# A fixed 56-step plan for the work woven into attention, and one modulation chunk moved to VectorE

## The chip, the cores and the metric

One core of one Trainium2 chip runs the whole program. The metric is the device time of one execution in microseconds. Three runs of the kernel before took 1927.2 us in the median (1920.5 to 1932.17).

The engines named below: TensorE (PE) multiplies matrices into PSUM, and its weight loads (PEld) run beside its products; VectorE (DVE), ScalarE (ACT) and GpSimd (POOL) work on tiles; SyncE (SP) issues the DMAs from one queue.

## What is computed

A block of two layers over 512 latent tokens and a context prefix of 256 tokens, model width 1024. Layer 0 mixes tokens by grouped-query attention (16 heads of 64, 4 key heads), layer 1 by a bidirectional Mamba-2 scan. Each layer ends with a gated feed-forward network of width 2816 with a depthwise convolution (FFN 0 and FFN 1). Shift, scale and gate of every sub-layer come from a linear map of the condition, for latent and for context rows: six chunks of 1024 numbers for each layer, for each of two conditions. Cut to what bears on the change:

```python
for i in range(DEPTH):
    need_ctx_out = i < DEPTH - 1
    mod_l = jnp.split((silu_c @ ada_w[i] + ada_b[i])[:, None, :], 6, axis=-1)
    mod_c = jnp.split(silu_cc @ ada_w[i] + ada_b[i], 6, axis=-1)
    h_l = modulate(rms_norm(x, norm_mix_w[i]), mod_l[0], mod_l[1])
    h_c = modulate(rms_norm(ctx, norm_mix_w[i]), mod_c[0], mod_c[1])
    ...
    x = x + mod_l[2] * o_l
    if need_ctx_out:
        ctx = ctx + mod_c[2] * o_c
    h_l = modulate(rms_norm(x, norm_ffn_w[i]), mod_l[3], mod_l[4])
    x = x + mod_l[5] * conv_ffn(h_l, ...)
    if need_ctx_out:
        h_c = modulate(rms_norm(ctx, norm_ffn_w[i]), mod_c[3], mod_c[4])
        ctx = ctx + mod_c[5] * conv_ffn(h_c, ...)
return x
```

In layer 1 the context stream ends after the mixer's input, so its chunks 2 to 5 for context rows (`mod_c[2]` to `mod_c[5]`) are read by nothing.

## The kernel before

Activations lie transposed, features on the 128 partitions, tokens along the free axis. Every product with a weight is made three times, from a high and a low part of both factors (`mm3`, L105, L106, L108); a weight of 128 x 1024 is loaded by SP, its high part is a cast on ScalarE (L85) and its low part a subtraction (L87), on VectorE or, with `lo_engine="pool"`, on GpSimd. Weights and the modulation's slabs share one pool of 10 tiles (`t4`); a load waits until a tile is free.

**Attention** runs its eight head pairs in seven steps each, 56 in all. A step makes the scores of one key tile (L686, L688), their exponential on ScalarE (L689), a running sum on VectorE (L694, L696), the products with the values of the step before (L650), and one piece of the next pair's row maxima: a product (L614) and a reduction on VectorE (L616). `final` closes a pair: sums on TensorE (L656), then VectorE and ScalarE (L659 to L663). The scores and the maxima share two PSUM buffers.

**Woven into the steps** are other jobs, as Python generators that `Fill` advances. After each step `fill.run(us)` spends a budget of 1.75 us (2.9 us in the last two pairs) by going through the queue in order and drawing from each generator as long as budget is left; a `BREAK` rests a generator for some steps. The queue is `"123a4k5a6a7aaaaa"`:

- digits are `queries(p)`: for pairs 4 to 7 load and split of the weight, 16 units of products (`ps_q`), and for all pairs the chain `normed`: a square and a scaling on ScalarE (L527, L528), four small SBUF-to-SBUF loads that swap rows (`qsw`, L531), the rotary products (L532 to L534) on the engine that the caller names, GpSimd here, sums of squares on TensorE (L540), and the normalisation (L546 to L552); last the split into a high and a low part;
- `k` is the same chain for the second pair of key heads (`keys(1)`);
- each `a` is one of eight modulation jobs `ada` for chunks 2 to 5 of layer 0: four loads of 512 KB, 8 products (`ps_ada`, L128), a copy to SBUF (L130), 4 transposes (`ps_adt`, L134), the bias added (`modulation`).

`fill.require` runs to its end what the next pair needs. Pairs 0 to 5 write their output to DRAM (`odram`). In the first step of pair 6 five of them are fetched back and split (`osplit`) and two output projections are queued (`late`, `project`: groups (0,1,2) and (3,4) of `w_o`), each adding to `X` on VectorE (`down`, L797). The group (5,6,7) follows behind the attention, merged with the first products of FFN 0.

Instructions of all engines are placed by a scheduler that takes the program's order as priority; on its engine, an instruction runs in the order so found.

**FFN 0** (`ffn`): 22 blocks of two products each (`up`: gate, then value), convolution and gating on VectorE and ScalarE, and `down` in groups of blocks (`segs`: nine of 2, one of 1, one of 3), whose updates multiply by `mod[0][5]`. Between them `side` puts the modulation of layer 1 on VectorE: `ada_dve` sums each of 48 loaded tiles against the latent and the context condition (L167, 96 sums), one sum at each place.

Of the kernel before, what the change touches and what calls it, by code (L numbers as in the profile page):

```python
# [7 lines left out]
P = 128  # L8
# [102 lines left out]
def ada(g, src, layer, chunks, m0, nm, big=True):  # L111
# [23 lines left out]
    for i, ch in enumerate(chunks):  # L135
        modulation(g, pt[:, 2 * nm * i : 2 * nm * (i + 1)], layer, ch, m0, nm)
# [3 lines left out]
def modulation(g, ps, layer, ch, m0, nm):  # L140

    nc = g.nc
    c0 = PC[f"adab{layer}"] + ch * KT + m0
    md = g.mod[layer][ch][:, m0 : m0 + nm, :]
    nc.vector.tensor_tensor(md, ps.rearrange("p (m v) -> p m v", v=2),
                            g.par[:, c0 : c0 + nm].unsqueeze(2).broadcast_to([P, nm, 2]), ALU.add)
    if ch in (1, 4):
        n0 = PC[("nmix" if ch == 1 else "nffn") + str(layer)] + m0
        nc.vector.scalar_tensor_tensor(g.moda[layer][ch][:, m0 : m0 + nm, :], md, 1.0,
                                       g.par[:, n0 : n0 + nm].unsqueeze(2).broadcast_to([P, nm, 2]),  # L150
                                       ALU.add, ALU.mult)


def ada_dve(g, layer):
# [5 lines left out]
    for ch in range(6):  # L160
        md = g.mod[layer][ch]
        for m in range(KT):
            w = g.t3p.tile([P, D], F32, tag="wada", bufs=3, name="wada")
            nc.sync.dma_start(w, g.I["adaT"][ch * KT + m])
            for v in range(2):
                junk = g.t3p.tile([P, D], F32, tag="junk", bufs=1, name="junk")
                g.tc.keep_in_program_order(nc.vector.scalar_tensor_tensor(  # L167
                    junk, w, 1.0, cb[:, v * D : (v + 1) * D], ALU.mult, ALU.mult, accum_out=md[:, m, v : v + 1]))
                yield
        modulation(g, md.rearrange("p m v -> p (m v)"), layer, ch, 0, KT)  # L170
# [5 lines left out]
class Fill:  # L176

    def __init__(self):  # L180
        self.q, self.cool, self.left = [], {}, 0.0

    def add(self, gen):
        self.q.append(gen)

    def run(self, us):

        self.left = min(self.left, 0.0) + us
        self.cool = {g: n - 1 for g, n in self.cool.items() if n > 1}
        for g in list(self.q):  # L190
            while self.left > 0 and g not in self.cool:
                r = next(g, None)
                if r is None:
                    self.q.remove(g)
                    break
                if r is BREAK:
                    self.cool[g] = 3
                    self.left -= 1.0
                else:
                    self.left -= r  # L200

    def require(self, gen):
        for _ in gen:
            pass
        if gen in self.q:
            self.q.remove(gen)

    def drain(self):
        for g in self.q:
            for _ in g:  # L210
                pass
        self.q = []
# [166 lines left out]
def attention(g, fill, X, late):  # L379
# [144 lines left out]
    def normed(qs, gain, eng):  # L524
# [7 lines left out]
        eng.tensor_tensor(qs[:, :L], qs[:, :L], g.cos, ALU.mult)  # L532
        eng.tensor_tensor(sw, sw, g.sin, ALU.mult)
        eng.tensor_tensor(qs[:, :L], qs[:, :L], sw, ALU.add)  # L534

# [6 lines left out]
        yield BREAK  # L542
# [10 lines left out]
        yield BREAK  # L553
# [3 lines left out]
    def keys(j, qs, eng):  # L557
        yield from normed(qs, kn, eng)
# [9 lines left out]
        yield 0  # L568
# [3 lines left out]
    def queries(p, qs, eng):  # L572
        if qs is None:
            w = load_w(g, I["wq"][p - 4], lo_engine="pool")
            yield BREAK
            qs = t3(g, "qs")
            for h, c0, n in ((hc, L, C), (hl, 0, L)):
                ps = Bk("ps_q")
                for k in range(KT):
                    ks = slice(k * P, (k + 1) * P)  # L580
                    mm3(g, (w[0][:, ks], w[1][:, ks]), [(ps[:, :n], h[k])], k == 0, k == KT - 1)
                    yield 3 * n / 2400
                nc.scalar.copy(qs[:, c0 : c0 + n], ps[:, :n])
            yield BREAK
        yield from normed(qs, g.qn8, eng)
        qprep[p] = t3(g, "qh", F32R), t3(g, "ql", F32R)
        split(g, qs, *qprep[p])
        yield 0
# [118 lines left out]
    for n, j in enumerate((0, 1, 2, 4, 5, 3)):  # L707
# [6 lines left out]
        if n in (1, 2):  # L714
            early.append(keys(0, raw[0], nc.vector) if n == 1 else queries(0, raw[1], nc.vector))
# [7 lines left out]
    qgen = {p: queries(p, raw[{1: 2, 2: 4, 3: 5}[p]] if p < 4 else None, nc.gpsimd) for p in range(1, 8)}  # L723
    kgen = keys(1, raw[3], nc.gpsimd)

    g.oT = []
    odram = [g.dp.tile([P, T], F32, name=f"odram{p}") for p in range(6)]

    def osplit(p):
        hl_, hc_ = htiles(g, L, f"ol{p}"), htiles(g, C, f"oc{p}")  # L730
        o = g.o[p]
        if p < 6:
            o = t3(g, f"od{p}")
            nc.sync.dma_start(o, odram[p])
        split(g, o[:, :L], *hl_)
        split(g, o[:, L:T], *hc_)
        g.oT.append((hl_, hc_))

    adas = list(fill.q)
    fill.q = [kgen if o == "k" else adas.pop(0) if o == "a" else qgen[int(o)] for o in "123a4k5a6a7aaaaa"]  # L740
    g.o = []
    pairs = [Pair(p) for p in range(NH // 2)]

    m = pairs[0].maxima()
    for i, _ in enumerate(vals):
        if i % 5 == 0:
            next(m, None)
        if i % 6 == 5:
            next(qgen[1], None)
    for _ in m:  # L750
        pass
    late_step = None
    for p in range(NH // 2):
        m = iter(())
        if p < 7:
            fill.require(qgen[p + 1])
            if p == 3:
                fill.require(kgen)
            m = pairs[p + 1].maxima()
        us = 1.75 if p < 6 else 2.9  # L760
        for t, todo in enumerate(pairs[p].steps()):
# [694 lines left out]
```

## Time and profile before

| what | value |
|---|---|
| median of 3 runs | 1927.2 us |
| the profiled execution: its span | 1929.7 us |
| bytes read from HBM | 198.79 MB |
| DMA, share of 16 engines' time | 34.0% |

The page gives the execution's span, from the first to the last instruction, and no other time of it. An engine's share is its busy time over the span. A busy TensorE is not one at its peak: products are pipelined, and the clock that it is granted is a row of its own. In the timeline's rows the bracket gives the idle time ahead of an instruction and what ended it.

### The profile page before, as it was taken

What the parts mean: (1) busy time and instruction counts of PE and PEld (TensorE: products, weight loads), DVE (VectorE), ACT (ScalarE), POOL (GpSimd) and SP (SyncE); (2) the same over time, 40 slices, a digit from 0 to 9 for tenths busy, and PEclk for the clock granted to TensorE, in tenths of its full rate; (3) what the DMA queues carried; (4) which work ended last, traced back from release to release, by engine and by line L of the source; (5) the groups of instructions that cost most, each with busy time, mean ns of one, the idle gap of its engine ahead of it and who ended that gap; (6) DMA issues with size and microseconds to landing.
All of it is one profiled execution on the core that took longest, in us unless ns stands there. A gap on an engine that the chain in (4) does not pass through costs nothing.

```text
span 1929.7 us, 27392 instructions
## 1 busy us (share of the span) xinstructions
PE 1877.4 (97%) x10744; PEld 1533.9 (79%) x10744; DVE 1337.2 (69%) x1976; ACT 844.2 (44%) x1446; POOL 312.5 (16%) x274
## 2 busy tenths in 40 slices
PE   8989999999999999999999999999999999999999
PEld 6755544678888888888888888888888878888887
DVE  5577777768777777775577777777878466555555
ACT  3655444345222222222256777766677343333331
POOL 2241101022000000000031334443335210000000
PEclk9989998999999999999999999999999999999999
DMA  8221343104434443332222444344343322323332
GB/s 334 77 88 37 124 150 128 45 23 143 128 123 131 131 131 122 121 95 62 68 92 63 132 117 124 110 131 120 106 136 120 99 77 88 109 88 101 97 99 87
DMA packets 73424, 210.00 MB, mean 109 GB/s; under 512 B 8912, under 2 KB 14416, under 8 KB 73168
## 3 DMA queue, kind: packets, MB, share of 16 engines
q1 hardware_dynamic: 73296, 208.26, 34.0%
q8 instruction: 84, 1.38, 0.3%
q14 instruction: 44, 0.36, 0.1%
HBM read 198.79 MB, written 6.82 MB: 107 GB/s over the span
## 4 chain that ended last, share of the span: by engine, by line
PE 77%; DVE 8%; ACT 4%; issue 3%; POOL 2%; DMA 2%; SPq 0%; POOLq 0%; DVEq 0%; ACTq 0%
PE ps_up L108 10%; PE ps_up L106 10%; PE ps_up L105 10%; PE ps_d L105 6%; PE ps_d L106 6%; PE ps_d L108 6%; PE ps_in L108 4%; PE ps_in L106 4%; PE ps_in L105 4%; PE ps_o L650 2%; PE ps_s L686 2%; PE ps_st L1043 2%; PE ps_wo L108 1%; DVE ht L281 1%; PE ps_wo L105 1%
## 5 line engine op out<-in xcount | busy, mean ns | idle before, releaser
L87 DVE TENSOR_TENSOR wl<-wst,wh 128x1024 fp32r<-128x1024 f32 x205 | 255.4, 1246 | 222.8 <-PE ps_up L106 110.1
L85 ACT CAST wh<-wst 128x1024 fp32r<-128x1024 f32 x211 | 221.2, 1049 | 411.7 <-DMA wst<-in_wup 336.6
L106 PE MATMUL ps_up<-hlf,wh 128*128 128x512 f32 x1008 | 357.1, 354 | 0.0
L105 PE MATMUL ps_up<-hhf,wh 128*128 128x512 f32 x1008 | 356.9, 354 | 0.0
L108 PE MATMUL ps_up<-hhf,wl 128*128 128x512 f32 x1008 | 356.8, 354 | 0.0
L106 PEld LDWEIGHTS ps_up<-hlf,wh 128*128 128x128 f32 x1008 | 190.6, 189 | 26.2
L105 PEld LDWEIGHTS ps_up<-hhf,wh 128*128 128x128 f32 x1008 | 190.6, 189 | 26.2
L108 PEld LDWEIGHTS ps_up<-hhf,wl 128*128 128x128 f32 x1008 | 190.5, 189 | 25.9
L105 PE MATMUL ps_in<-hhs,wh 128*128 128x512 f32 (+1 forms) x560 | 204.4, 365 | 0.0
L106 PE MATMUL ps_in<-hls,wh 128*128 128x512 f32 (+1 forms) x560 | 199.4, 356 | 0.0
L108 PE MATMUL ps_in<-hhs,wl 128*128 128x512 f32 (+1 forms) x560 | 198.7, 355 | 0.0
L105 PE MATMUL ps_d<-hdh,wh 128*128 128x512 f32 (+1 forms) x568 | 193.7, 343 | 1.4 <-DVE X L797 1.2
L108 PE MATMUL ps_d<-hdh,wl 128*128 128x512 f32 (+1 forms) x568 | 193.4, 341 | 0.0
L106 PE MATMUL ps_d<-hdl,wh 128*128 128x512 f32 (+1 forms) x568 | 192.9, 340 | 0.3 <-DVE hdl L87 0.3
L797 DVE SCALAR_TENSOR_TENSOR X<-ps_d,mod,X 128x512 f32<-128x512 f32 (+1 forms) x240 | 132.9, 588 | 20.8 <-PE ps_d L108 20.4
L106 PEld LDWEIGHTS ps_d<-hdl,wh 128*128 128x128 f32 x568 | 106.7, 188 | 15.5 <-DVE hdl L87 0.7
L105 PEld LDWEIGHTS ps_d<-hdh,wh 128*128 128x128 f32 x568 | 106.3, 188 | 15.4 <-DVE X L797 1.7
L105 PEld LDWEIGHTS ps_in<-hhs,wh 128*128 128x128 f32 x560 | 105.9, 189 | 15.1 <-issue 1.2
L167 DVE SCALAR_TENSOR_TENSOR junk<-wada,cb 128x1024 f32<-128x1024 f32 x96 | 117.2, 1220 | 1.1 <-ACT cb L159 0.9
L108 PEld LDWEIGHTS ps_in<-hhs,wl 128*128 128x128 f32 x560 | 105.8, 189 | 14.7
L108 PEld LDWEIGHTS ps_d<-hdh,wl 128*128 128x128 f32 x568 | 106.7, 188 | 13.3
L106 PEld LDWEIGHTS ps_in<-hls,wh 128*128 128x128 f32 x560 | 106.0, 189 | 13.2
(344 smaller groups left out, 3525.0 us busy)
## 6 DMA issues: line engine op xcount, KB each, us to landing
wst<-in_wup SPq DMA_DIRECT2D x88, 512.0 KB, 3.6
wada<-in_adaT SPq DMA_DIRECT2D x48, 512.0 KB, 3.6
wst<-in_win SPq DMA_DIRECT2D x48, 512.0 KB, 3.6
wst<-in_wdown SPq DMA_DIRECT2D x44, 512.0 KB, 4.2
wada<-in_adaB SPq DMA_DIRECT2D x32, 512.0 KB, 5.2
E<-ad SPq DMA_DIRECT2D x64, 256.0 KB, 7.3
ec<-ead SPq DMA_DIRECT2D x64, 128.0 KB, 5.1
wst<-in_wout SPq DMA_DIRECT2D x16, 512.0 KB, 3.5
```

Of the source, the lines that this page charges most:

```text
L85: keep(nc.scalar.copy(hi, src))
L87: keep(eng.tensor_tensor(lo, src, _r(hi), ALU.subtract))
L105: mm(out, wh, ah, start=first, stop=False)
L106: mm(out, wh, al, start=False, stop=False)
L108: mm(out, wl, ah, start=False, stop=last)
L167: g.tc.keep_in_program_order(nc.vector.scalar_tensor_tensor(junk, w, 1.0, cb[:, v * D : (v + 1) * D], ALU.mult, ALU.mult, accum_out=md[:, ...
L281: nc.vector.scalar_tensor_tensor(t[:, c0:c1], ap, g.moda[layer][ca][:, m, v : v + 1], rs[:, c0:c1], ALU.mult, ALU.mult)
L650: nc.tensor.matmul(po[S64[e], :n], v, pr[:, 512 * e + off : 512 * e + off + n], start=first, stop=last)
L686: nc.tensor.matmul(outs[e], a[S64[e], k], b[S64[e], q], start=i == 0, stop=False)
L797: nc.vector.scalar_tensor_tensor(ap, o[:, c0:c1], gate[:, m, v : v + 1], ap, ALU.mult, ALU.add)
L1043: nc.tensor.matmul(ps[:, d * 256 : (d + 1) * 256], Bt[:, t * P : (t + 1) * P], xw[d][t], start=t == ts[0], stop=t == ts[-1])
```

## The change

- `Fill` is replaced by `Weave`, which knows the 56 steps. At each step it takes all charges still open, divides them by the steps left, and spends that much. `Job`s are units of TensorE work with a charge; up to three places ahead in the list a job may do its loads. `Light`s are short pieces without products of weight (a part of a chain, one split), at most one at each step, with an earliest step and a condition. Loads of `w_o` and of the outputs are in a list of their own (`free`), three steps ahead of their splits.
- The rotary products and the query weights' low parts go from GpSimd to VectorE. In `normed` they stand behind the sums of squares.
- The weight of pair 4 is loaded ahead of the value loop and split at its unit 20; the chain of pair 1 is finished before the steps.
- The outputs are split one by one from step 31 on instead of five at once in the first step of pair 6; the projections are grouped (0,1), (2,3,4), then (5,6,7) as before.
- Six modulation jobs instead of eight run on TensorE. Chunk 5 of layer 0 is summed in `ada_dve`, ahead of layer 1, at two sums for each place in the first four blocks of FFN 0, so that it is there for the first `down`; the first group has 3 blocks, and the one of 1 is gone. Chunks 2 to 5 of layer 1 are summed for the latent condition alone: 16 + 32 + 32 = 80 sums instead of 96.

```diff
+    def step(self):
+        todo = sum(j.cost for j in self.jobs) + sum(it.cost for it in self.lights)
+        self.left = min(self.left, 0.0) + todo / max(1, self.steps - self.now)
+        self.left -= self.light()
+        for i, j in enumerate(self.jobs[:3]):
+            if i <= j.ahead:
+                j.start(self.now)
+        for j in list(self.jobs):
+            while self.left > 0 and j.cool <= self.now and not j.prep and j.ready():
+                r = next(j.units, None)
...
-    def normed(qs, gain, eng):
+    def normed(qs, gain):
...
-        eng.tensor_tensor(qs[:, :L], qs[:, :L], g.cos, ALU.mult)
-        eng.tensor_tensor(sw, sw, g.sin, ALU.mult)
-        eng.tensor_tensor(qs[:, :L], qs[:, :L], sw, ALU.add)
...
+        nc.vector.tensor_tensor(qs[:, :L], qs[:, :L], g.cos, ALU.mult)
+        nc.vector.tensor_tensor(sw, sw, g.sin, ALU.mult)
+        nc.vector.tensor_tensor(qs[:, :L], qs[:, :L], sw, ALU.add)
+        yield
...
-            w = load_w(g, I["wq"][p - 4], lo_engine="pool")
...
+    def wq_split(p):
+        wh, wl = t4(g, "wh", F32R), t4(g, "wl", F32R)
+        split(g, wq[p], wh, wl)
+        wq[p] = (wh, wl)
...
-    fill.q = [kgen if o == "k" else adas.pop(0) if o == "a" else qgen[int(o)] for o in "123a4k5a6a7aaaaa"]
...
+    weave = Weave(7 * len(pairs))
...
+        return Job(2.95, units(), lambda: next(gen), ahead=1)
...
+        jobs[p] = Job(8.35, q_units(p), lambda p=p: wq_load(p), lambda p=p: isinstance(wq.get(p), tuple))
...
+        jobs[fs] = Job(8 * len(fs) * 1.05, project(fs, wo), None,
+                       lambda fs=fs: all(f in g.oT and isinstance(wo.get(f), tuple) for f in fs))
...
+    weave.jobs = [jobs[4], a[0], jobs[5], a[1], jobs[6], a[2], jobs[7], a[3], a[4], a[5], jobs[0, 1], jobs[2, 3, 4]]
...
+        for i in range(3):
+            its.append(Light(lambda: next(gen, None), at, cost=0.0 if i else 1.45,
+                             ready=(lambda now: ready()) if i == 0 else
+                             (lambda now, b=its[i - 1], d=3 - i: b.when is not None and now >= b.when + d)))
...
+    wsplit = lambda p: Light(lambda: wq_split(p), 0, lambda now: jobs[p].began is not None and now >= jobs[p].began + 2)
+    q2, q3, kk = chained(2, 0), chained(3, 5), chained("k", 13)
+    qc = {p: chained(p, at, lambda p=p: jobs[p].done) for p, at in ((4, 9), (5, 20), (6, 29), (7, 36))}
...
-            if t == 0:
-                if p == 6:
-                    for i in range(5):
-                        osplit(i)
-                    late()
...
-            fill.run(us)
...
+    def place(f):
+        for _ in range(2 if f < 4 else 1):
+            next(side, None)
...
-    for n in [2] * 9 + [1, 3] if nxt else [2] * 11:
+    for n in [3] + [2] * 8 + [3] if nxt else [2] * 11:
...
-    for i in range(8):
-        fill.add(ada(g, I["adaB"][i], 0, (2 + i // 2,), 4 * (i % 2), 4))
+    adas = [ada(g, I["adaB"][i], 0, (2 + i // 2,), 4 * (i % 2), 4) for i in range(6)]
```

More of the change, by code (lines that the diff above doesn't have):

```diff
@@ L168, in ada_dve, with __init__, start @@
                     junk, w, 1.0, cb[:, v * D : (v + 1) * D], ALU.mult, ALU.mult, accum_out=md[:, m, v : v + 1]))
+                if layer == 0 and m == KT - 1 and v == 1 or layer and m == KT - 1 and v == nv - 1:
+                    break
                 yield
-        modulation(g, md.rearrange("p m v -> p (m v)"), layer, ch, 0, KT)
+        modulation(g, md[:, :, 0:nv], layer, ch, 0, KT, nv)
+        yield
 BREAK = object()
[L176 to L192, printed above, removed]
+class Job:
+    def __init__(self, cost, units, prep, ready=lambda: True, ahead=2):
+        self.cost, self.units, self.prep, self.ready, self.ahead = cost, units, prep, ready, ahead
+        self.began = None
+        self.cool, self.done = 0, False
+    def start(self, now=0):
+        if self.prep:
+            self.prep()
+            self.prep, self.began = None, now
@@ new lines, with __init__, light @@
+class Weave:
+    def __init__(self, steps):
+        self.jobs, self.lights, self.now, self.steps, self.left, self.n = [], [], 0, steps, 0.0, 0
+    def light(self):
+        for it in self.lights:
+            if it.at <= self.now and it.ready(self.now):
+                self.lights.remove(it)
+                it.run()
+                it.when = self.now
+                return it.cost
+        return 0.0
+    def step(self):
[8 more added lines that the diff above has]
+                r = next(j.units, None)
@@ L744, in attention @@
+    qfirst = chain[1]
+    jobs[4].start()
     m = pairs[0].maxima()
@@ L748, in attention @@
         if i % 6 == 5:
-            next(qgen[1], None)
+            next(qfirst, None)
+        if i == 20:
+            wq_split(4)
     for _ in m:
+        pass
+    for _ in qfirst:
         pass
```

189 lines of the change are left out of this document (113 added, 76 removed).

## The prediction

> **What bounds the kernel now.** I read the page first: the span, the engines' shares, the strip of the granted clock, the chain that ended last.
>
> ```profile
> span 1929.7 us, 27392 instructions
> PE 1877.4 (97%) x10744; PEld 1533.9 (79%) x10744; DVE 1337.2 (69%) x1976; ACT 844.2 (44%) x1446; POOL 312.5 (16%) x274
> ...
> PEclk9989998999999999999999999999999999999999
> ...
> PE 77%; DVE 8%; ACT 4%; issue 3%; POOL 2%; DMA 2%; SPq 0%; POOLq 0%; DVEq 0%; ACTq 0%
> ```
>
> TensorE is busy 97% of the span and makes 77% of the chain: a change is worth TensorE work taken out, or TensorE waits and slow clock taken out. The clock strip dips in slices of 48 us that include 96 to 145 and 289 to 338. So the view of windows is next, by stage: the attention steps run from 116 (first scores) to 411, FFN 0 from 460 to 975.
>
> ```profile
> 116.00:411.00 295.00, 279.20 (x1674) 157.41 (x1673) 219.40 (x302) 128.69 (x172) 41.73 (x25) 0.96 0.28 95
> ...
> 327.00:370.00 43.00, 42.24 (x239) 28.04 (x240) 35.41 (x54) 13.79 (x20) 0.00 (x0) 1.00 0.13 44
> ...
> 460.00:975.00 515.00, 514.78 (x2981) 454.30 (x2979) 360.69 (x556) 127.66 (x134) 0.11 (x1) 1.00 0.37 116
> ```
>
> Columns: length, then busy time of PE, PEld, DVE, ACT, POOL, then the granted clock. FFN 0 has 0.2 us of idle TensorE at full clock: nothing that leaves VectorE there can shorten it. The attention steps have 295.0 - 279.2 = 15.8 us of idle TensorE and a mean clock of 0.96. The timeline of TensorE gives the idle times with what ended them:
>
> ```profile
> 125.38 0.80 PE L686 MATMUL ps_s<-qh,kh 64*128 64x512 f32 x2 [4.09 <-ACT pr L689]
> 129.24 1.98 PE L650 MATMUL ps_o<-pr,v 128*64 128x512 f32 x4 [1.37 <-DVE qsq L550]
> ...
> 188.87 1.08 PE L656 MATMUL ps_sum<-acc,ones 128*64 128x512 f32 x4 [2.40 <-DVE qsq L550]
> ...
> 272.26 0.50 PE L686 MATMUL ps_s<-qh,kh 64*128 64x512 f32 x2 [2.06 <-ACT pr L689]
> ...
> 306.46 0.80 PE L614 MATMUL ps_m<-kh,qh 64*128 64x256 f32 x4 [2.62 <-DVE ma L616]
> ```
>
> These five are 12.54 us of the 15.8; the other 3.3 are shorter waits. The clock falls behind three of the five (windows of 4 us):
>
> ```profile
> 124.00:128.00 4.00, 2.50 (x10) 1.50 (x10) 2.65 (x1) 3.88 (x6) 3.51 (x2) 0.65 0.00 0
> 128.00:132.00 4.00, 2.76 (x8) 0.50 (x12) 4.00 (x6) 0.52 (x1) 0.00 (x0) 0.50 0.38 131
> 132.00:136.00 4.00, 4.00 (x20) 0.69 (x12) 1.77 (x3) 0.83 (x1) 0.00 (x0) 0.57 0.42 142
> ...
> 188.00:192.00 4.00, 3.13 (x16) 1.72 (x18) 3.72 (x8) 1.97 (x3) 0.00 (x0) 0.76 0.00 0
> 192.00:196.00 4.00, 4.00 (x20) 2.35 (x17) 3.59 (x7) 1.69 (x4) 0.00 (x0) 0.82 0.02 4
> ...
> 304.00:308.00 4.00, 1.53 (x5) 0.79 (x6) 4.00 (x5) 1.78 (x2) 0.00 (x0) 0.76 0.72 289
> 308.00:312.00 4.00, 4.00 (x16) 2.71 (x16) 2.55 (x4) 0.00 (x0) 0.00 (x0) 0.50 0.00 0
> 312.00:316.00 4.00, 4.00 (x11) 1.10 (x8) 1.90 (x3) 1.83 (x3) 0.00 (x0) 0.50 0.00 0
> ```
>
> Busy time times the missing clock: 2.50 x 0.35 + 2.76 x 0.50 + 4.00 x 0.43 = 4.0 us behind the first wait; 0.8 + 0.7 = 1.5 behind the third; 0.4 + 2.0 + 2.0 = 4.4 behind the last. So the five waits cost 12.5 + 9.9 = 22.4 us, and the attention steps are where time can be had.
>
> What made them, from the timeline of the other engines:
>
> ```profile
> 122.62 1.04 ACT L85 CAST wh<-wst 128x1024 fp32r<-128x1024 f32 x1 [1.86 <-DMA wst<-in_wq]
> ...
> 125.36 3.23 DVE L694 TENSOR_TENSOR acc<-pr 128x1024 f32<-128x1024 f32 x1 [1.51 <-ACT pr L689]
> ...
> 306.32 0.95 DVE L87 TENSOR_TENSOR ql<-qs,qh 128x768 fp32r<-128x768 f32 x1
> ```
>
> At 122.6 the cast of a query weight stood on ScalarE waiting for its load, with the step's exponential behind it; at the same time a VectorE addition took 3.23 us while GpSimd was busy 3.51 of 4.00. At 304 to 308 VectorE is busy 4.00 of 4.00: weight splits, a query split and the pair's own sums meet where five outputs and their weights are taken back at once.
>
> **The change, part by part.**
>
> ```profile
> 201.71 1.92 PE L128 MATMUL ps_ada<-wada,sc 128*32 128x512 f32 x16
> ...
> 209.13 1.08 PE L650 MATMUL ps_o<-pr,v 128*64 128x512 f32 x4
> ...
> 211.50 1.08 PE L650 MATMUL ps_o<-pr,v 128*64 128x512 f32 x4
> ...
> 213.94 1.05 PE L134 MATMUL ps_adt<-cst,ada_sb 128*128 128x2 f32 x8
> ...
> 217.21 1.03 PE L656 MATMUL ps_sum<-acc,ones 128*64 128x512 f32 x4
> ```
>
> *Two of eight modulation jobs leave TensorE.* One job is 1.92 us of products and 1.05 us of transposes, so 2 x 2.97 = 5.9 us of TensorE work leave a stage that TensorE bounds.
>
> *They come back in FFN 0* as 16 VectorE sums, at two per place for the first four blocks, and 32 sums for context rows that nothing reads are dropped.
>
> ```profile
> L167 DVE SCALAR_TENSOR_TENSOR junk<-wada,cb 128x1024 f32<-128x1024 f32 x96 | 117.2, 1220 | 1.1 <-ACT cb L159 0.9
> ```
>
> VectorE there gets 16 x 1.22 = 20 us more and 39 us less, in 515 us of which it works 361. Four blocks take four sums each instead of two: 8 x 1.22 = 9.8 us more in the first 60 us. TensorE's own 515 us cover it; I take 0, and 9.8 us as the upper end if it comes onto the path. Eight more loads of 512 KB go to a DMA share of 0.37. Grouping the down projection by three first and no group of one keeps every product and saves a pass of updates on VectorE, under the same cover: 0.
>
> *Spread and lookahead.* Query weights are loaded when the job is two places off and split two steps later; the early split lies in the value loop; output reloads and splits lie one per step instead of five at once; the three parts of a query's chain are set two and one steps apart. The waits at 125 and 306 have the two causes shown; those at 129 and 188 end with a step of a query's chain on VectorE (L550), that at 272 with an exponential that came late. All five are of work that the plan sets apart, so I count all 22.4 us as gone and leave the other 3.3 us as they are. What is late next is VectorE.
>
> *GpSimd's part moves to VectorE*: three rotary products for each of seven chains and four weight splits.
>
> ```profile
> L533 DVE TENSOR_TENSOR qsw<-qsw,cs x2: 680/684/687, 77.3 to 83.5; 128x512 f32<-128x512 f32 x2
> ...
> L87 DVE TENSOR_TENSOR wl<-wst,wh 128x1024 fp32r<-128x1024 f32 x205 | 255.4, 1246 | 222.8 <-PE ps_up L106 110.1 <-ACT wh L85 78.3 <-issue 17.3
> ```
>
> 21 x 0.684 + 4 x 1.246 = 19.3 us on VectorE: 219.4 + 19.3 = 239 us. In steps of 295 - 24 = 271 us that is 88%. From 327 to 370 VectorE was at 35.41 / 43 = 82% while TensorE lost 0.8 us at clock 1.00; 88% is somewhat beyond that row. Losing the collisions with GpSimd (3.23 us for an addition) gives some of it back; I count neither.
>
> *A wait is added.* The rotary products overwrite the tile that four small loads read, so VectorE waits for all four, and the pair's maxima and sums are queued behind; TensorE's next maxima wait for them. On GpSimd nothing stood behind it. In before, the first chain already runs on VectorE, ahead of the steps:
>
> ```profile
> 76.62 0.78 DVE L532 TENSOR_TENSOR raw<-raw,cs 128x512 f32<-128x512 f32 x1 [11.17 <-DMA qsw<-raw]
> ...
> 82.86 0.69 DVE L532 TENSOR_TENSOR raw<-raw,cs 128x512 f32<-128x512 f32 x1 [0.70 <-DMA qsw<-raw]
> ...
> L531 SPq DMA_DIRECT2D qsw<-qs x16: 507/582/593, 171.4 to 290.5; - x16
> ...
> DMA to landing us min/median/max: 1.9/3.1/5.9
> ```
>
> Four issues on SP's queue and a landing are 3 x 0.58 + 3.1 = 4.8 us from the first issue. Bounds for one chain: 0, if the queue holds other ready work ahead, and 4.8. The 11.17 is a VectorE with nothing else to do; the 0.70 of the second chain, with other work in the queue, is the nearest row. I take 0.7 x 7 = 4.9 us, all on the path.
>
> Sum: 22.4 + 5.9 - 4.9 = 23.4 us. 1929.7 - 23.4 = 1906.3 for the span. The page gives no time of its execution beside the span; the runs shown have a median of 1927.2, 2.5 us lower, so the forecast is **1904 us**.
>
> One rule of the Trainium skill is weighed here. "TensorE: Matmul & The Clock Gate", Part 1, says that the array falls to half clock after an idle window of some 3.4 us. By that, waits of 2.40 and 2.62 us should cost no clock, and the gain would be 5.9 us smaller; this trace shows 0.76 and 0.50 behind them, so the rows decide.
>
> **The rivals.**
>
> *VectorE stands at the rotary loads* (the other side). The place is the first part of each chain. If VectorE waits the full 4.8 us less two ready operations of 1.2 us ahead of it, 7 x 2.4 = 17 us take the place of 4.9: 1916. If it waits all 4.8 us and the clock falls behind each wait as at 188 (1.5 us), 7 x 6.3 = 44 us stand against 28.3: 1943. From 28.3 / 7 = 4.0 us a chain on, the change loses. For: nothing can pass on VectorE. Against: 0.70 us at 82.86, and TensorE has a step's other work to run meanwhile. Chance 0.17, of which 0.06 faster by over 0.5%, 0.05 within, 0.06 slower. "TensorE: Matmul & The Clock Gate" of the Trainium skill gives VectorE, in its table of the engine, a strict first-in-first-out queue; no run here shows one instruction passing another, so the page speaks for this rival.
>
> *The plan doesn't do what it says*: stalls move instead of going, since VectorE's 239 us are spread evenly and every pair is as full as 289 to 327 was. Then only the 5.9 us of taken-out work come: 1927.2 - 5.9 = 1921. For: VectorE's share rises from 74% to 88%. Against: the 82% stretch ran clean. Chance 0.13.
>
> *Better than the sum*: the steps run with no stall. A bare step is 211.50 - 209.13 = 2.37 us; 56 x 2.37 = 133, the plan's own charges are 103 (6 jobs of 2.95, 4 of 8.35, 42 for the projections, 7 chains of 1.45; the first agrees with 2.97 above), and the sums add 8 x 1.03 = 8: 244 us against 295, so 1876 at the lower end.
>
> **How the numbers follow.** Forecast, with the better case as its lower part: 0.70, own range 1880 to 1915. Doubled pace in FFN 0 on the path adds at most 9.8 us inside it. First rival 0.17, second 0.13. Half a per cent is 9.6 us, about what a measurement of this kernel can tell from no change. Faster: 0.70 + 0.06 = 0.76; within: 0.13 + 0.05 = 0.18; slower 0.06. The range for 8 in 10 reaches to the second rival and a little over: 1880 to 1925.
>
> **What would show it.** Right: in the windows of the new trace the attention steps take about 272 us, idle TensorE is under 10 us, the clock is 0.99 or more throughout, VectorE is at 85 to 90%, and FFN 0 is 515 us as before. Rotary products with VectorE idle ahead of them, ended by the small loads, for several us each would show the first rival; the same idle time spread over more and shorter waits on VectorE the second. A longer first 60 us of FFN 0 would show the doubled pace. The forecast is wrong in its main step if the five waits are gone and the steps still take over 285 us.

## The result and the profile after

The changed kernel took 1909.95 us in the median of six executions (1905.23 to 1912.46), the kernel before beside it 1920.88 us (1919.84 to 1932.17). The ratio is 0.9924, with a 95% interval of 0.99 to 0.9948. In a second comparison (six executions against 17, further down) it was 0.9918 [0.99, 0.9936]. The forecast was 1904 us.

The page of the changed kernel; its profiled execution took 1909.82 us, 1.8 us more than its span:

```profile
span 1908.0 us, 27239 instructions
...
PE 1864.2 (98%) x10696; PEld 1527.1 (80%) x10696; DVE 1321.9 (69%) x1953; ACT 844.5 (44%) x1446; POOL 263.8 (14%) x246
...
PEclk8999999999999999999999999999999999999999
...
PE 79%; DVE 9%; issue 4%; ACT 2%; POOL 1%; DMA 1%; SPq 0%; DVEq 0%; POOLq 0%; ACTq 0%
```

The span is 21.7 us shorter than the 1929.7 of before, the two dips in the clock strip at attention are gone, and ScalarE's 4% of the chain of waits has become 2%. Where the time went is in the windows (length, then busy time of PE, PEld, DVE, ACT, POOL, then the granted clock): the attention steps, FFN 0, and its first 60 us.

```profile
119.00:392.00 273.00, 265.15 (x1628) 150.11 (x1624) 224.05 (x322) 130.34 (x176) 0.00 (x0) 0.99 0.26 86
441.00:956.00 515.00, 514.59 (x2986) 454.69 (x2985) 337.07 (x510) 128.45 (x134) 0.05 (x1) 1.00 0.39 124
...
441.00:501.00 60.00, 60.00 (x353) 53.31 (x352) 48.16 (x73) 22.97 (x24) 0.05 (x1) 1.00 0.55 185
```

The steps take 273 us instead of 295, with 273.00 - 265.15 = 7.85 us of idle TensorE instead of 15.8, at a clock of 0.99 instead of 0.96. GpSimd does nothing there. FFN 0 has TensorE busy throughout, its first 60 us included, where chunk 5 now comes in. The 22 us are all from the steps. From the first scores (`ps_s`) to the last sums (`ps_oc`) they take 292.4, 289.1 and 288.2 us in three profiles of the kernel before and 270.1 and 268.9 in two of the changed kernel; the further profiles are among the experiments below.

The longest idle times of TensorE left in the steps, from its timeline:

```profile
151.55 3.61 PE L128 MATMUL ps_ada<-wada,sc 128*32 128x512 f32 x16 [1.43 <-DVE qsq L580]
...
170.50 1.05 PE L134 MATMUL ps_adt<-cst,ada_sb 128*128 128x2 f32 x8 [0.84 <-DVE qsq L580]
...
256.35 1.05 PE L128 MATMUL ps_ada<-wada,sc 128*32 128x512 f32 x4 [1.72 <-DMA wada<-in_adaB]
...
316.20 0.39 PE L105 MATMUL ps_d<-hhoc,wh 128*128 128x256 f32 x1 [0.89 <-DVE X L897]
```

All five waits that the prediction listed are gone. Four others stand there, 4.9 us together: a step of a chain on VectorE twice, a modulation slab that has not landed, an update of `X`. In windows of 4 us the clock falls in only one place of the steps:

```profile
148.00:152.00 4.00, 1.91 (x13) 0.98 (x17) 3.91 (x10) 1.26 (x3) 0.00 (x0) 0.95 0.04 17
152.00:156.00 4.00, 4.00 (x23) 0.98 (x17) 2.39 (x5) 0.36 (x1) 0.00 (x0) 0.63 0.36 95
```

Busy time times the missing clock gives 0.1 + 1.5 = 1.6 us here, against 9.9 in the profile of before. The view of waits (engine, line, for what: us in total, times, longest) has the wait that was feared most:

```profile
PEld ps_ada L128 <- DMA wada<-in_adaB: 4.6, 4, 2.6
...
DVE raw L569 <- DMA qsw<-raw: 3.7, 2, 3.0
```

VectorE waited twice at the small loads of the rotary products, 3.7 us in all, and none of TensorE's longer waits ends on `raw`. The shorter of the two, 0.66 us at 145.35, does open a nearly unbroken run of VectorE work that ends with the `qsq` of TensorE's 1.43 us wait, so the rotary products have a share in that one.

### The profile page after: what moved, and what is told of

It reads as the page before. It is cut to its first block, busy times and chain, and to the rows that moved or that the text cites. A ratio compares the mean times of both kernels' runs of the same rounds, so it can differ in the third digit from the quotient of the medians.

```text
span 1908.0 us, 27239 instructions
## 1 busy us (share of the span) xinstructions
PE 1864.2 (98%) x10696; PEld 1527.1 (80%) x10696; DVE 1321.9 (69%) x1953; ACT 844.5 (44%) x1446; POOL 263.8 (14%) x246
## 4 chain that ended last, share of the span: by engine, by line
PE 79%; DVE 9%; issue 4%; ACT 2%; POOL 1%; DMA 1%; SPq 0%; DVEq 0%; POOLq 0%; ACTq 0%
PE ps_up L106 10%; PE ps_up L108 10%; PE ps_up L105 10%; PE ps_d L105 6%; PE ps_d L108 6%; PE ps_d L106 6%; PE ps_in L108 4%; PE ps_in L106 4%; PE ps_in L105 4%; PE ps_o L687 2%; PE ps_s L723 2%; PE ps_st L1147 2%; DVE ht L312 1%; PE ps_wo L108 1%; PE ps_wo L105 1%
## 5 line engine op out<-in xcount | busy, mean ns | idle before, releaser
L87 DVE TENSOR_TENSOR wl<-wst,wh 128x1024 fp32r<-128x1024 f32 x209 | 260.4, 1246 | 243.3 <-PE ps_up L106 137.5
L897 DVE SCALAR_TENSOR_TENSOR X<-ps_d,mod,X 128x512 f32<-128x512 f32 (+1 forms) x224 | 124.9, 583 | 34.1 <-PE ps_d L108 33.6
L726 ACT ACTIVATE pr<-ps_s 128x1024 f32<-128x1024 f32 x56 | 57.1, 1020 | 97.5 <-PE ps_s L725 95.6
```

The source lines that it names most:

```text
L87: keep(eng.tensor_tensor(lo, src, _r(hi), ALU.subtract))
L726: nc.scalar.activation(pr, ps, AF.Exp)
L897: nc.vector.scalar_tensor_tensor(ap, o[:, c0:c1], gate[:, m, v : v + 1], ap, ALU.mult, ALU.add)
```

## The experiments

The change has three parts: the plan (P), the modulation part (M: six jobs on TensorE, chunk 5 in FFN 0, unused sums left out) and the GpSimd part (G: rotary products and low parts of query weights to VectorE). In the table each ratio is to executions of the kernel before beside it. "Clock" is the mean granted clock over a kernel's executions; "time x clock" is the mean over its executions of time times clock, an estimate of what would be left if TensorE, which is nearly always at work, had never been slowed. The standard error of that mean is 0.2 to 0.6 us in the rows, 1.3 in that of P + M.

| kernel | label | executions | median us (range) | ratio [95%] | clock | time x clock |
|---|---|---|---|---|---|---|
| before | e0_before | 12 | 1924.9 (1917.6 to 1929.7) | 1.0 [0.9984, 1.0015] | 0.992 | 1909.9 |
| before + M | e5_m | 12 | 1922.0 (1918.4 to 1930.0) | 0.9986 [0.9969, 1.0003] | 0.991 | 1906.4 |
| before + G | e4_g | 12 | 1922.1 (1918.8 to 1925.8) | 0.9982 [0.9967, 0.9997] | 0.993 | 1909.3 |
| before + M + G | e6_mg | 12 | 1923.8 (1917.2 to 1927.8) | 0.9991 [0.9973, 1.0008] | 0.991 | 1905.9 |
| P alone | e3_p | 8 | 1916.9 (1914.2 to 1922.7) | 0.9962 [0.9944, 0.9979] | 0.995 | 1907.6 |
| P + G | e1_gp | 6 | 1911.8 (1908.7 to 1915.5) | 0.9935 [0.9909, 0.9961] | 0.995 | 1902.9 |
| P + M | e2_mp | 6 | 1910.5 (1909.1 to 1912.6) | 0.9929 [0.9901, 0.9956] | 0.994 | 1898.8 |
| P + M + G, the changed kernel | e10_after | 6 | 1910.8 (1906.4 to 1912.9) | 0.9918 [0.99, 0.9936] | 0.994 | 1898.1 |
| before, value weights' low parts on VectorE | e9_bwv | 12 | 1919.6 (1917.1 to 1928.5) | 0.9973 [0.9957, 0.9988] | 0.994 | 1908.8 |
| changed, value weights' low parts on VectorE | e7_wv | 6 | 1908.4 (1906.4 to 1909.9) | 0.9916 [0.9891, 0.9941] | 0.994 | 1897.1 |
| the same, slabs loaded two places ahead | e8_ahead | 5 | 1906.7 (1903.2 to 1906.9) | 0.9895 [0.9877, 0.9914] | 0.995 | 1895.6 |

**The kernel before again.** No edit.

> The kernel before once more, for a second profile. The profiled execution that the prediction used had a span of 1929.7 us, while four of six executions took 1919.8 to 1921.3 and two 1927.2 and 1932.2. Theory A (the cost of the attention steps' waits differs between executions): where the execution is one of the short ones, the attention steps take 284 to 287 us instead of 295, with fewer waits or less slow clock behind them, and every other stage is as long as it was, within 1 us. Rival B: the steps take 295 us again and the 10 us are missing in another stage (the values' products ahead of the steps, FFN 0, or the scan). Time: within 0.3% of the kernel before by either.

Its 12 executions agree with the others of the kernel before. The one that was profiled took 1929.68 us and was not a short one, so it can't tell theory A from rival B. It shows four of the first profile's five waits again (4.12, 1.52, 2.40 and 2.06 us); the fifth is 0.58 us. In the steps it loses 8.9 us to the slow clock, and 3.2 of them at a place where no wait stands ahead:

```profile
288.00:292.00 4.00, 3.78 (x30) 1.22 (x28) 3.49 (x7) 3.42 (x6) 0.00 (x0) 1.00 1.02 417
292.00:296.00 4.00, 4.00 (x38) 3.10 (x34) 2.63 (x6) 1.83 (x3) 0.00 (x0) 1.00 0.86 250
296.00:300.00 4.00, 4.00 (x19) 2.01 (x19) 3.91 (x7) 1.96 (x2) 3.61 (x3) 0.69 0.37 112
300.00:304.00 4.00, 4.00 (x20) 1.35 (x20) 1.35 (x4) 0.00 (x0) 1.27 (x1) 0.50 0.99 314
```

In the 8 us before 296 TensorE is idle for 0.22 us; a modulation job's products and transposes are among what it runs there.

In 77 executions of the kernel before that ran beside the experiments, these 12 among them, the median is 1925.1 us and the range 1917.6 to 1933.3: nearly 16 us, against 8 in the 12 of the changed kernel. The spread goes with the granted clock: 1919.04 us at 0.995, 1924.50 at 0.994, 1933.30 at 0.987. Over the 77, time against time times (1 - clock) has a correlation of 0.94 and a slope of 0.91.

**The plan alone.** M and G undone in the changed kernel. The unused sums of layer 1 stay left out, and the doubled pace and the first group of three in FFN 0 stay too:

```diff
-    for layer, ch in [(0, 5)] + [(1, c) for c in range(6)]:
+    for layer, ch in [(1, c) for c in range(6)]:
...
-        nc.vector.tensor_tensor(qs[:, :L], qs[:, :L], g.cos, ALU.mult)
+        eng.tensor_tensor(qs[:, :L], qs[:, :L], g.cos, ALU.mult)
...
-        split(g, wq[p], wh, wl)
+        split(g, wq[p], wh, wl, lo_engine="pool")
...
-    weave.jobs = [jobs[4], a[0], jobs[5], a[1], jobs[6], a[2], jobs[7], a[3], a[4], a[5], jobs[0, 1], jobs[2, 3, 4]]
+    weave.jobs = [jobs[4], a[0], jobs[5], a[1], jobs[6], a[2], jobs[7], a[3], a[4], a[5], a[6], a[7], jobs[0, 1], jobs[2, 3, 4]]
```

> The plan alone: rotary products and the query weights' low parts go back to GpSimd, all eight modulation jobs run on TensorE in the steps. Theory A (the plan takes out the waits, the moved work little): about 5.9 us slower than the changed kernel, so 1914 to 1917 against 1921 of before. Rival C (the gain comes from the modulation jobs that left and from GpSimd leaving VectorE alone; the plan only moves waits): 1920 to 1922, no faster than before.

1916.9 us, inside theory A's range: the plan alone gives about 8 us, about half of the whole. Most of it is clock (0.992 to 0.995): in time x clock 2.3 us remain. From the first scores to the last sums TensorE is idle for 10.8 us, against 15.7, 13.9 and 14.7 in the three profiles of the kernel before, and the clock is 1.00 throughout. So the plan by itself takes out the slow clock and only some of the idle time. Its timeline of TensorE shows waits that are new:

```profile
153.41 0.50 PE L725 MATMUL ps_s<-diag,onesr 64*128 64x512 f32 x2 [2.89 <-DVE diag L674]
...
186.98 0.50 PE L725 MATMUL ps_s<-diag,onesr 64*128 64x512 f32 x2 [1.39 <-DVE diag L674]
...
249.38 1.05 PE L128 MATMUL ps_ada<-wada,sc 128*32 128x512 f32 x4 [0.75 <-DMA wada<-in_adaB]
...
273.11 1.05 PE L128 MATMUL ps_ada<-wada,sc 128*32 128x512 f32 x4 [1.18 <-DMA wada<-in_adaB]
...
296.31 1.05 PE L128 MATMUL ps_ada<-wada,sc 128*32 128x512 f32 x4 [0.79 <-DMA wada<-in_adaB]
```

The last three are 2.7 us: eight jobs of the plan ask for slabs faster than they land. Ahead of the first, VectorE's low part of a query (`ql`) took 2.50 us instead of some 0.95 beside a subtraction on GpSimd.

**The modulation part alone**, on the kernel before:

```diff
-    fill.q = [... for o in "123a4k5a6a7aaaaa"]
+    fill.q = [... for o in "123a4k5a6a7aaa"]
...
-    for n in [2] * 9 + [1, 3] if nxt else [2] * 11:
+    for n in [3] + [2] * 8 + [3] if nxt else [2] * 11:
```

with the new `ada_dve` and `place` of the change.

> The kernel before with the modulation part alone: six jobs on TensorE instead of eight, chunk 5 of layer 0 summed in FFN 0 at the doubled pace, the context sums of layer 1 that nothing reads left out, the first group of three. Theory A: 1 to 5.9 us faster than before (1915 to 1920); FFN 0 as long as before, 515 us. Rival C: 6 us or more faster (1915 or less). If the doubled pace is on the path, FFN 0 is up to 9.8 us longer and the time is that of before or longer.

**The GpSimd part alone**, on the kernel before:

```diff
-            w = load_w(g, I["wq"][p - 4], lo_engine="pool")
+            w = load_w(g, I["wq"][p - 4])
...
-    kgen = keys(1, raw[3], nc.gpsimd)
+    kgen = keys(1, raw[3], nc.vector)
```

and the same for `qgen`.

> The kernel before with the GpSimd part alone: rotary products and the query weights' low parts on VectorE, the old queue of jobs. Theory A: VectorE gets 19 us more and stands at the small loads in the old bursts; no faster than before, 1920 to 1930. Rival C: the collisions of GpSimd and VectorE were the cost, so 3 to 8 us faster, 1913 to 1918.

**Both, without the plan**, the two edits together:

> The kernel before with the modulation part and the GpSimd part, without the plan. If the parts add: 0.9986 and 0.9982 alone give 0.9968. If the plan is needed for VectorE to take the work: 0.998 to 1.0.

M alone has a median 2.9 us below the repeated kernel before, G alone 2.8, both together 1.1; of the three intervals only that of G leaves out 1.0, by little. M's share fits theory A, though its interval includes 1.0. G's median lies in theory A's range and not in the rival's 1913 to 1918, so the collisions on VectorE were not the main cost; nor is G a loss. Both together fit the second case, 0.998 to 1.0. In time x clock M is worth 3.5 us, G 0.6 and both 4.0, so they add up there; the medians differ by their clocks (0.991, 0.993, 0.991).

**The changed kernel without M** (its two jobs back on TensorE, chunk 5's sums out of FFN 0) **and without G** (three rotary products and the low parts back on GpSimd); the edits are those of the plan alone, one half each.

> The changed kernel with its modulation part undone: all eight jobs on TensorE in the steps, chunk 5 of layer 0 not summed in FFN 0 (the doubled pace in the first four blocks stays, for layer 1's sums). Theory A (each part adds its own share): slower than the changed kernel by the 2.7 us that the part brought alone, up to the 5.9 us of TensorE work: a ratio to before of 0.994 to 0.996. Rival D (with VectorE fuller, TensorE work in the steps is free): ratio 0.992 to 0.993, as the changed kernel.

> The changed kernel with its GpSimd part undone: rotary products and the query weights' low parts on GpSimd again, plan and modulation as changed. The prediction's own step: VectorE gets 19 us less and does not stand at the small loads, so 0 to 5 us faster than the changed kernel (ratio 0.990 to 0.992). Rival E (a VectorE instruction that starts beside a GpSimd one lasts until that ends, so GpSimd costs VectorE more than it takes over): 3 to 6 us slower than the changed kernel (ratio 0.994 to 0.996).

Without M the ratio of 0.9935 lies between the two forecasts and decides nothing; without G the kernel is as fast as with it, which speaks against rival E and leaves the prediction's own step at its lower end, 0.

On top of the plan M is worth 1916.9 - 1910.5 = 6.4 us in medians and 8.8 in time x clock; the latter is near the sum of the 5.9 us of work and the 2.7 us of slab waits that the plan alone had. On plan and G it is worth less: 1911.8 - 1910.3 = 1.5 us in medians and 1902.9 - 1898.7 = 4.2 in time x clock. G on the plan gives 5.1 in medians and 4.7 in time x clock, on plan and M nothing (1910.5 and 1898.8 without, 1910.3 in 12 executions and 1898.7 with). Nowhere does it cost the 4.9 us forecast. So on the plan M alone brings what both bring (8.8 against 8.9 in time x clock) and G alone 4.7: their shares don't add up.

**The front: two value weights off GpSimd.** Ahead of the steps the changed kernel's first values (`ps_v`) started at 93.9 us with a wait of 5.66, in the first profile of before at 90.9. The edit, on the changed kernel and on the kernel before:

```diff
-            wv.append(load_w(g, I["wv"][len(wv)], lo_engine="pool", pin=True))
+            wv.append(load_w(g, I["wv"][len(wv)], pin=True))
```

> The changed kernel with the low parts of the two value weights on VectorE instead of GpSimd, ahead of the steps. In the changed kernel's trace a VectorE subtraction of 0.94 us lasts 3.15 us beside GpSimd's 2.64 us, and TensorE then waits 5.66 us for the first values' product, at a clock of 0.69 and 0.88 after it. If that collision is the cause: the wait falls to 3 us or less, the products begin at 91 us or earlier instead of 93.9, and the time is 3 to 6 us below the changed kernel (ratio to before 0.989 to 0.991). If the wait is of the ScalarE chain in any case: no difference.

> The kernel before with one edit: the value weights' low parts on VectorE instead of GpSimd. If a VectorE instruction is held up beside GpSimd ahead of the attention steps in the kernel before too, this alone gives 1.5 to 3 us (median about 1922 against some 1924.5). If that collision is the changed kernel's alone (in the kernel before, the key's low part took 0.94 us there), the median stays within 1 us of the kernel before.

The changed kernel gains about 2 us (1910.3 to 1908.4; 1898.7 to 1897.1), less than the 3 to 6 expected; its wait is 2.92 us, as expected, and the products begin at 91.8. The kernel before gains more, and more than the 1.5 to 3 expected: 0.9973 [0.9957, 0.9988], some 5 us, though on TensorE, ScalarE and SP every instruction stands in its old place and two subtractions change engine (on GpSimd the order of some instructions of the scan in layer 1 is another, too). In time x clock it gains 1.1; the rest is clock, 0.992 to 0.994. TensorE in the steps of that kernel, timeline and windows:

```profile
126.87 0.50 PE L686 MATMUL ps_s<-qh,kh 64*128 64x512 f32 x2 [3.15 <-ACT pr L689]
...
186.72 1.08 PE L656 MATMUL ps_sum<-acc,ones 128*64 128x512 f32 x4 [2.40 <-DVE qsq L550]
...
268.50 0.50 PE L686 MATMUL ps_s<-qh,kh 64*128 64x512 f32 x2 [2.07 <-ACT pr L689]
...
301.68 0.50 PE L614 MATMUL ps_m<-kh,qh 64*128 64x256 f32 x4 [1.59 <-DVE ma L616]
```

```profile
188.00:192.00 4.00, 4.00 (x28) 2.78 (x27) 3.78 (x5) 3.41 (x6) 0.00 (x0) 1.00 0.02 4
192.00:196.00 4.00, 4.00 (x23) 1.91 (x23) 4.00 (x8) 1.32 (x2) 0.00 (x0) 1.00 0.25 98
...
304.00:308.00 4.00, 4.00 (x19) 1.68 (x19) 3.52 (x5) 1.84 (x3) 0.00 (x0) 1.00 0.00 1
```

The wait of 2.40 us is there to the hundredth, and those of 2.07 and 1.59, but no slow clock stands behind any of these three. The 1.4 us of slow clock in its steps stand behind the first wait, 3.15 us (0.91 and 0.66 from 124 to 132).

**The kernel before once more**, for another profile of the same program:

> The kernel before, unchanged, for one more profile. If the waits belong to the order of the work and the slow clock behind them to the moment of the execution, TensorE shows the waits of about 4.1, 1.4, 2.4 and 2.1 us again in the same places of the attention steps, while the windows of 4 us with a granted clock under 0.95 in the steps are other ones than the eight of the first profile (124 to 136, 188 to 196, 304 to 316), and the time is about 1911 us plus the time times one minus its mean clock (1920 at 0.995, 1930 at 0.990). If the slow clock belongs to the waits, it falls behind the same ones, by as much.

This execution took 1934.01 us. Its timeline, and its windows with a low clock in the steps (those at 128 to 140 left out):

```profile
131.29 0.62 PE L686 MATMUL ps_s<-qh,kh 64*128 64x512 f32 x2 [4.18 <-ACT pr L689]
135.29 1.97 PE L650 MATMUL ps_o<-pr,v 128*64 128x512 f32 x4 [1.67 <-DVE qsq L550]
...
193.42 1.98 PE L656 MATMUL ps_sum<-acc,ones 128*64 128x512 f32 x4 [2.40 <-DVE qsq L550]
...
278.14 0.68 PE L686 MATMUL ps_s<-qh,kh 64*128 64x512 f32 x2 [2.06 <-ACT pr L689]
...
312.57 0.50 PE L614 MATMUL ps_m<-kh,qh 64*128 64x256 f32 x4 [1.24 <-DVE ma L616]
```

```profile
192.00:196.00 4.00, 2.58 (x8) 0.88 (x10) 3.50 (x10) 0.56 (x1) 0.00 (x0) 0.62 0.00 0
196.00:200.00 4.00, 4.00 (x21) 2.17 (x18) 3.10 (x5) 2.52 (x5) 0.00 (x0) 0.53 0.02 4
276.00:280.00 4.00, 1.94 (x11) 1.40 (x10) 3.23 (x3) 2.92 (x4) 0.00 (x0) 0.79 0.14 56
280.00:284.00 4.00, 4.00 (x28) 0.97 (x28) 2.36 (x2) 1.02 (x1) 0.00 (x0) 0.79 0.00 0
```

Same program, nearly the same waits (the last is 1.24 us instead of 2.62), another clock. Behind the 2.06 us wait, which cost no clock in the first profile (1.00 from 268 to 276), it falls to 0.79; behind the one at 312 it doesn't fall. Behind the first wait and that of 2.40 us it falls in all three profiles of this kernel, by other amounts. So the first four waits belong to the order of the work, and how much slow clock stands behind a wait, if any, to the execution. By busy time times missing clock the steps lose 9.9 us in the first profile, 8.9 in that of e0_before, 6.5 here and 1.4 in the kernel with the value weights on VectorE. Ahead of the steps, by the same reckoning, the three profiles of the kernel before lose 3.1, 7.6 and 9.0 us, and the two of the changed kernel 6.0 and 7.6: of the same order, and not looked at in the prediction.

The front differs between executions too. VectorE's, GpSimd's and TensorE's timeline in the first profile of before:

```profile
84.07 0.94 DVE L565 TENSOR_TENSOR kl<-raw,kh 64x768 fp32r<-64x768 f32 x1
84.44 2.85 POOL L87 TENSOR_TENSOR wl<-wst,wh 128x1024 fp32r<-128x1024 f32 x1 [7.58 <-ACT wh L85]
84.94 2.89 DVE L534 TENSOR_TENSOR raw<-raw,qsw 128x512 f32<-128x512 f32 x1
...
90.86 0.42 PE L516 MATMUL ps_v<-wh,hha 128*128 128x256 f32 x1 [2.98 <-ACT raw L711]
```

and in this one:

```profile
87.08 2.63 POOL L87 TENSOR_TENSOR wl<-wst,wh 128x1024 fp32r<-128x1024 f32 x1 [7.57 <-ACT wh L85]
...
87.37 3.15 DVE L565 TENSOR_TENSOR kl<-raw,kh 64x768 fp32r<-64x768 f32 x1
...
96.18 0.58 PE L516 MATMUL ps_v<-wh,hha 128*128 128x256 f32 x1 [5.65 <-ACT raw L711]
```

The VectorE instruction that starts while GpSimd's subtraction runs ends only after it, by 0.5 us in the first rows and 0.8 in the second. If `kl` starts first, a rotary product is held (2.89 us instead of some 0.68) and TensorE waits 2.98 us; if GpSimd starts first, `kl` is held (3.15 instead of 0.94), ScalarE waits 2.75 us for it with its next copies behind, and TensorE waits 5.65. Both orders were seen in both kernels (TensorE's wait in the changed one was 5.66 us in the first profile and 3.27 in the repeat). In the eleven profiles with these low parts on GpSimd, `kl` is first in seven (TensorE's wait 2.63 to 3.27 us) and GpSimd in four (5.65 to 5.72); in the three with them on VectorE the wait is 2.92 to 3.47. Four of eleven at 2.7 us makes an estimate of 1.0 us for the move, near the 1.1 of time x clock in the kernel before. The steps began at 115.8, 117.6 and 121.6 us in three profiles of the kernel before and at 118.7 and 119.0 in two of the changed one, so the 2.9 us by which they began later in the first pair can't be put down to the change. "GPSIMD Engine Reference" of the Trainium skill, section 8, says that GpSimd shares its SBUF interfaces with VectorE and contends with VectorE instructions of two SBUF inputs; the rows agree, and the price on them is 2.2 us (2.89 - 0.68, 3.15 - 0.94), nearly the 2.3 that were left of the GpSimd instruction.

**The changed kernel again, and slabs loaded earlier.**

> The changed kernel once more, beside the two others: 1908 to 1912 us, and executions that spread over less than 8 us, if the spread of the kernel before (14 us) comes from the waits in its steps that are gone here. A spread of 10 us or more would say that the spread has another source.

```diff
-        return Job(2.95, units(), lambda: next(gen), ahead=1)
+        return Job(2.95, units(), lambda: next(gen), ahead=2)
```

on the changed kernel with the value weights on VectorE:

> The changed kernel with the value weights' low parts on VectorE (median 1908.4 us), and a modulation job's loads started up to two places ahead in the list instead of one. If the waits that are left in the steps at modulation slabs (4.6 us before four weight loads of TensorE in the changed kernel) lie on the path, they go, and the median is 1904 to 1906 us. If the four loads only change places with those of the query weights and the output projections, the median stays at 1907 to 1910 us.

The repeat took 1910.8 us and spreads over 6.5 us, both as expected. With the earlier loads 1906.7 us, between the two ranges forecast and 1.8 below the kernel without them (time x clock 1.5 below). The two ranges overlap by 0.5 us, so this is likely and not certain; in its profile no wait of TensorE for a slab of 0.6 us or more is left in the steps. It is the fastest kernel of all, 0.9895 [0.9877, 0.9914], some 4 us below the changed one.

## Why the prediction was right, and where it was not

The direction and the range held, and so did the mechanism in the main: waits and slow clock leave the attention steps, two modulation jobs leave TensorE, FFN 0 covers what comes to it. The size came short: some 15 to 16 us (medians of 1925.1 and 1910.3, or 0.9918 of 1926.6), 11 in the first comparison, where 23.4 were forecast.

**The sum fits the one execution it was made against.** Its span fell by 21.7 us. The steps fell by 22, where 272 us were forecast for them and 273 came, at the forecast clock of 0.99 and with under 10 us of idle TensorE.

**The step that failed is the term "9.9 us" of slow clock, and with it the line "the runs shown have a median of 1927.2, 2.5 us lower".** The clock behind the waits was taken as a property of the kernel, read from one execution. That execution had 1929.7 us of span at a mean clock of 0.990; the mean of the 77 is 0.992, and the steps lost 8.9 and 6.5 us of clock in two other profiled executions and, with two instructions on another engine, 1.4. The largest piece, "4.4 behind the last", is in neither of the two: there the last wait is 0.58 and 1.24 us, and the clock behind it is 1.00. The line on the median took the span for the time; in the runs the time is 1.8 us above the span (1909.82 and 1908.0, 1934.01 and 1932.2), which makes an estimate of 1931.5 us for this execution, 6.4 above the median of the 77. It was a long one, and its whole slow clock was subtracted from a median. Against many executions the clock gave 4.5 us: time less time x clock is in the mean 15.5 us before (1925.4 - 1909.9) and 11.0 after (1909.7 - 1898.7). The rest of the change is 1909.9 - 1898.7 = 11.2 us, where 12.5 + 5.9 - 4.9 = 13.5 were forecast. The two together are 15.7.

**"I count all 22.4 us as gone" put too much on the plan.** Alone it gives about 8 us, 2.3 in time x clock, and most of the idle time moves to other places. M and G on top of it bring 6.6 us in medians and 8.9 in time x clock, where 5.9 - 4.9 = 1.0 was forecast. That the total came nearer than its parts is luck: a plan priced too high and a loss that didn't come offset each other.

What remains slow after has other places. The rule weighed in the prediction, that of an idle window of some 3.4 us, goes on in the Trainium skill ("TensorE: Matmul & The Clock Gate", Part 1) with the statement that the window is free-running and does not start with the kernel. That sentence was not used, and it bears on the failed step: by it the same wait meets the window in another place in each execution. The rows agree in that the clock fell behind the 2.06 us wait in one of three profiles of the kernel before, and behind the 2.40 us wait in these three but not in that with the value weights on VectorE. They differ from the length that it gives: beside the waits of some 4.1 us, those of 1.43, 2.06, 2.40, 2.62 and 3.15 us cost clock too, and all of these are shorter. No run here shows the window itself.

**"12.5 us" of waits: the five went, but others came.** Idle TensorE in the steps fell by 15.8 - 7.85 = 8.0 us, not 12.5. The forecast had a loss of 4.9 beside the 12.5, so its net of 7.6 was near, for another reason than the one given: the new waits are at the chain's normalisation, a slab and `X`, not at the rotary loads. That is luck too.

**"5.9 us" for two modulation jobs** was right as work. On the plan M gave 8.8 in time x clock, with less waiting for slabs beside the work; on plan and G it gave 4.2.

**"-4.9 us" for the rotary products on VectorE was wrong.** VectorE waited 3.7 us in all, and G costs nothing on plan and M: with the rotary products on GpSimd (e2_mp) TensorE's wait at the place of the 1.43 us is 3.18. The 0.70 us that was multiplied by seven came from a front in which VectorE had just one other chain to do. VectorE's load was too high as well: 239 us were forecast for the steps and 224.05 came, 82% instead of 88%. Part of it is the collisions that "I count neither" left out. VectorE's groups of the steps, before:

```profile
L696 DVE TENSOR_TENSOR acc<-acc,pr 128x1024 f32<-128x1024 f32 x32 | 41.9, 1308 | 11.4 <-ACT pr L689 11.4
...
L694 DVE TENSOR_TENSOR acc<-pr 128x1024 f32<-128x1024 f32 x8 | 12.3, 1540 | 2.8 <-ACT pr L689 2.8
```

and after:

```profile
L733 DVE TENSOR_TENSOR acc<-acc,pr 128x1024 f32<-128x1024 f32 x32 | 39.0, 1217 | 9.0 <-ACT pr L726 9.0
...
L731 DVE TENSOR_TENSOR acc<-pr 128x1024 f32<-128x1024 f32 x8 | 9.7, 1217 | 1.1 <-ACT pr L726 1.1
```

The mean of one falls from 1308 and 1540 ns to 1217: 2.9 + 2.6 = 5.5 us come back on these two lines.

**FFN 0 at nothing** was right. In its first 60 us VectorE is busy 48.16 us and TensorE 60.00. The 80 sums are there, and 16 fewer than before:

```profile
L167 DVE SCALAR_TENSOR_TENSOR junk<-wada,cb 128x1024 f32<-128x1024 f32 x80 | 97.3, 1216 | 1.2 <-ACT cb L158 0.9
```

**The rivals.** VectorE stood at the rotary loads for 3.7 us, where the first rival needs 17 or more, so the queue's order cost little. The second rival, stalls that move instead of going, holds in part for the plan alone (10.8 us of idle TensorE left) and not for the whole change (7.85), which came well below its 1921. Without the plan M and G together gave 1.1 us in medians, on top of it 6.6 (1916.9 to 1910.3). That the steps run without any stall (1876) needed the last 7.85 us of idle TensorE and more.

**What stays open:** why the clock falls behind one wait and not behind its twin in another execution, why it falls at 296 us of e0_before without a wait ahead, and why the kernel before with two subtractions on VectorE keeps its clock more often.

## What to carry to other kernels

A gain that is read from slow clock in one profile holds for that execution: take the waits at full value, the clock behind them at what several executions of the same kernel show, and time x clock over many executions to tell the two apart. Before moving work off a shared helper engine is charged as load, count what its neighbour gets back, since a VectorE instruction beside a GpSimd one can last three times as long. Parts of a change that seem to give little alone can be worth more once the order of the work lets TensorE use it, and less again when another part has already taken the same idle time: here M was worth 3.5 us in time x clock alone, 8.8 on the plan and 4.2 on plan and G.

## What the runs showed of the hardware

- The granted clock fell to 0.50 to 0.82 for one to three windows of 4 us behind waits of TensorE of 1.43 to 4.18 us; behind the wait of 2.06 us it fell to 0.79 in one execution and stayed at 1.00 in two others of the same program; in one execution it fell to 0.69 and 0.50 with 0.22 us of idle TensorE in the 8 us ahead. The granted clock goes with most of a spread of 16 us between executions of one program on one core.
- A VectorE subtraction of 0.94 us took 3.15 us when GpSimd's of 2.63 us had started 0.3 us before it. Which of the two starts first differs between executions, and 2.7 us of TensorE's time hang on it (2.98 against 5.65).
